# Attention's key sets joined pair by pair of heads, bias tables written from all partitions, last pair last in the branch product

## The chip, the cores and the metric

The kernel runs on one core of a Trainium2 chip. The metric is the device time of one execution in microseconds (us). Three executions were timed, and their median counts; one further execution was profiled.

## The reference, cut to what matters

The kernel computes two transformer blocks over 512 tokens of width 1024. The change lies in the attention branch of the first block. It has 24 heads: three groups of 8, whose keys lie 1, 4 and 16 tokens apart. The outputs of the three groups are joined by a softmax over their log denominators, head by head and token by token; a branch product and a gate follow.

```python
logits = einsum('znqhd,znkhd->znhqk', qb, kw) * HEAD_DIM ** -0.5 + bias   # bias by bucketed distance
m = max(logits); p = exp(logits - m); den = sum(p)
o = einsum('znhqk,znkhd->znqhd', p, vw) / den;  lse = m + log(den)
...
alpha = softmax(stack(lses, axis=2), axis=2)
attn = sum(alpha[..., None] * o, axis=2)                                  # 512 x 512
...
merged = gates[:, :, 0] * (attn @ w_attn_branch) + gates[:, :, 1] * (ssm @ w_ssm_branch)
```

## The kernel before

Products run in three passes (`mm3`, L301 to L303, and `tok`, L384 to L386), because each operand is split into a high and a low part. A weight block of 512 KB is loaded by SP's queue into `wraw` (3 buffers), ScalarE (ACT) makes the high part `whi` (L292) and VectorE (DVE) the low part `wlo` (L293); a block feeds 24 matmuls of 512 columns.

`attention` does this in order:

- `rel_bias` (L428) makes the bias tables. One small product gives a row of 384, 256 or 256 numbers for each of 8 heads, on 8 partitions. A transfer on GpSimd's (POOL's) queue writes each row 128 times to DRAM (`scr<-p`: 1536, 1024 and 1024 KB); another reads it back with a pitch one element shorter, which skews it into the table by query and key (`B<-scr`, into B0 and B12).
- The V projection takes 12 weight blocks `w_v` and 288 matmuls.
- `qk` projects queries and keys of one pair of heads: 6 blocks.
- `units` does the attention of one pair of heads: two key sets (`sid` 0 is the group of step 1; `sid` 1 holds the groups of steps 4 and 16 together, its queries in the order quarter by quarter, that is tokens 0, 4, 8, ..., then 1, 5, 9, ...), each in two halves. Scores and bias are added and their maximum taken (L483, DVE), exponents and sums made (L492, ACT), the weights transposed (L499, PE) and multiplied with V (L514). Maxima and sums go into `st`, outputs into `Os`. The units of pair hp are interleaved with `qk` of pair hp + 1; those of the last pair with 5 of the 8 gate blocks (`gates`, L828), which need nothing from attention.
- `attn_join` (L581) comes once, after all four pairs, interleaved with the remaining 3 gates. It transposes `st`, sends it to DRAM (`dstat`), reads it back with heads on 8 partitions (`R`), works out the weights `W` of the two sets on [8, 512] rows, sends them to DRAM (`dw`), reads them back copied over 64 partitions a head (`Wb<-dw`, 8 transfers of 256 KB), and forms y = Os0 * W0 + Os1 * W1 for each pair. L317 and L318 split y into `ah` and `al`. All its transfers are on SP's queue.

The branch product in `block1_` then takes four blocks `w_ab` of 24 matmuls, two output tiles each; every output tile needs `ah` and `al` of all four pairs. The order of instructions on each engine is made at build time by a list scheduler with a cost model of its own; each engine then runs its list strictly in order.

Of the kernel before, what the change touches and what calls it, by code (L numbers as in the profile page):

```python
# [10 lines left out]
F32 = mybir.dt.float32  # L11
# [7 lines left out]
P = 128  # L19
# [230 lines left out]
class Kern:  # L250
# [177 lines left out]
    def rel_bias(self, pool):  # L428

        nc, D = self.nc, self.D  # L430
        B0 = pool.tile([P, 8, 256], F32, name="B0", bufs=1)
        B12 = pool.tile([P, 8, 256], F32, name="B12", bufs=1)

        flat = lambda: pool.tile([P, 2, 2, 256], F32, name="p").rearrange("p a b c -> p (a b c)")
        tab, es = flat()[:NBUCKET + 1, :896], flat()[:8]
        nc.gpsimd.dma_start(tab, D["btab"])
        lhs = self.small.tile([NBUCKET + 1, 24], F32, name="lhs", bufs=1)
        nc.vector.memset(lhs[NBUCKET:NBUCKET + 1], 1.0)
        nc.gpsimd.dma_start(lhs[0:NBUCKET], D["relb"])
        off = 0  # L440
        for g, L in enumerate((384, 256, 256)):
            ps = self.btile()[:8, :L]
            nc.tensor.matmul(ps, lhs[:, g * 8:(g + 1) * 8], tab[:, off:off + L], start=True, stop=True)
            e = es[:, off:off + L]
            off += L
            nc.vector.tensor_copy(e, ps)
            scr = self.dram.tile([8, P * L + 512], F32, name="scr%d" % g)
            dst = scr[:, :P * L].rearrange("h (p l) -> h p l", l=L)
            nc.gpsimd.dma_start(dst, e.unsqueeze(1).to_broadcast([8, P, L]))
            src = scr[:, :P * (L - 1)].rearrange("h (p l) -> p h l", l=L - 1)  # L450
            if g == 0:
                nc.gpsimd.dma_start(B0, src[:, :, 0:256])
            else:
                nc.gpsimd.dma_start(B12[:, :, (g - 1) * P:g * P], src[:, :, 0:P])
        return B0, B12

    def attn_unit(self, pool, hp, sid, half, qT, kT, V, bias, st, O):
# [9 lines left out]
        for u in range(2):  # L467
# [13 lines left out]
            for e in range(2):  # L481
                h = 2 * hp + e
                nc.vector.tensor_tensor_reduce(p[:, e, u, lo:], S[e][:, u, lo:], bias[:, h, lo:], 1.0, -3e38,  # L483
                                               op0=ALU.add, op1=ALU.max, accum_out=st[:, 2 * sid, h, i:i + 1])
        mx = st[:, 2 * sid, 2 * hp:2 * hp + 2, 2 * half:2 * half + 2]
        nc.vector.tensor_scalar(ng.rearrange("p (e u) -> p e u", e=2), mx, -1.0, None, op0=ALU.mult)
        for u in range(2):
            i = 2 * half + u
            lo = P if sid == 0 and i == 0 else 0
            for e in range(2):  # L490
                h = 2 * hp + e
                nc.scalar.activation(p[:, e, u, lo:], p[:, e, u, lo:], AF.Exp, bias=ng[:, 2 * e + u:2 * e + u + 1],  # L492
                                     accum_out=st[:, 2 * sid + 1, h, i:i + 1])
        yield
# [23 lines left out]
    def attention(self, xT, ah, al, other):  # L518
# [3 lines left out]
        with self.tc.tile_pool(name="ao", bufs=1) as op:  # L522
          st = op.tile([P, 4, 8, 4], F32, name="st")
          Os = op.tile([P, 4, 2, SEQ], F32, name="Os")
          with self.tc.tile_pool(name="at", bufs=2) as pool:
# [25 lines left out]

            def units(hp, qT, kT):

                last = None
                for sid in range(2):
                    O = self.psO.tile([P, SEQ], F32, name="pso")
                    for half in range(2):
                        u = self.attn_unit(pool, hp, sid, half, qT, kT, V, (B0, B12)[sid], st, O)
                        next(u)
# [11 lines left out]
            for hp in range(4):  # L571
                merge(units(hp, *qk_[hp]), qk(hp + 1, *qk_[hp + 1]) if hp < 3 else islice(other, 5))
          with self.tc.tile_pool(name="ac", bufs=2) as pool:
              merge(self.attn_join(pool, st, Os, ah, al), other)

    def attn_end(self, last, Os):
        _, hp, sid, half, O = last
        if half:
            self.nc.scalar.copy(Os[:, hp, sid], O)

    def attn_join(self, pool, st, Os, ah, al):  # L581

        nc = self.nc
        ps = self.btile()[:, :P]
        nc.tensor.transpose(ps, st.rearrange("p a b c -> p (a b c)"), self.ident)
        sT = pool.tile([P, P], F32, name="sT", bufs=1)
        nc.vector.tensor_copy(sT, ps)
        dst = self.dram.tile([4, 8, 4, P], F32, name="dstat")
        nc.sync.dma_start(dst.rearrange("a b c p -> (a b c) p"), sT)
        R = pool.tile([8, 4, SEQ], F32, name="R", bufs=1)  # L590
        nc.sync.dma_start(R, dst.rearrange("a b c p -> b a (c p)"))
        v = lambda i: R[:, i].rearrange("h (r i) -> h i r", r=4)
        n = lambda t: t.rearrange("h (i r) -> h i r", r=4)
        W = pool.tile([8, 2, SEQ], F32, name="W", bufs=1)
        tm = pool.tile([8, 2, SEQ], F32, name="tm", bufs=1)
        M, L = tm[:, 0], tm[:, 1]
        V_, S_ = nc.vector, nc.scalar
        yield
        V_.tensor_tensor(n(M), n(R[:, 0]), v(2), op=ALU.max)
        V_.tensor_tensor(W[:, 0], R[:, 0], M, op=ALU.subtract)  # L600
        V_.tensor_tensor(n(W[:, 1]), v(2), n(M), op=ALU.subtract)
        S_.activation(W, W, AF.Exp)
        V_.tensor_tensor(L, W[:, 0], R[:, 1], op=ALU.mult)
        V_.tensor_tensor(n(M), n(W[:, 1]), v(3), op=ALU.mult)
        V_.tensor_tensor(L, L, M, op=ALU.add)
        V_.reciprocal(L, L)
        V_.tensor_tensor(W, W, L.unsqueeze(1).to_broadcast([8, 2, SEQ]), op=ALU.mult)
        dw = self.dram.tile([8, 2, SEQ], F32, name="dw")
        nc.sync.dma_start(dw, W)
        yield  # L610
        for hp in range(4):
            Wb = pool.tile([P, 2, SEQ], F32, name="Wb")
            for e in range(2):
                nc.sync.dma_start(Wb[64 * e:64 * e + 64], dw[2 * hp + e].unsqueeze(0).to_broadcast([64, 2, SEQ]))
            y = pool.tile([P, SEQ], F32, name="ay")
            z = pool.tile([P, SEQ], F32, name="az")
            V_.tensor_tensor(y, Os[:, hp, 0], Wb[:, 0], op=ALU.mult)
            V_.tensor_tensor(n(z), Os[:, hp, 1].rearrange("d (r i) -> d i r", r=4), n(Wb[:, 1]), op=ALU.mult)
            V_.tensor_tensor(y, y, z, op=ALU.add)
            self.dump("attnT%d" % hp, y)  # L620
            self.split(ah[:, hp], al[:, hp], y)
            yield

# [228 lines left out]
    def block1_(self, keep, c1):  # L852
# [5 lines left out]
        with tc.tile_pool(name="b1", bufs=1) as pl:  # L858
# [13 lines left out]
            with tc.tile_pool(name="ahl", bufs=1) as ap_:  # L872
# [3 lines left out]
                with tc.tile_pool(name="gp", bufs=1) as gp:  # L876
                    gts = [gp.tile([P, SEQ], F32, name="g%d" % i) for i in range(8)]
                    self.attention(xT, ah, al, self.gates(xT, 0, gts))
                    for s in range(4):
                        w = self.wload(D["w_ab"], s, 1)  # L880
                        for j in range(2):
                            fb = 2 * s + j
                            ps = self.ptile()
                            self.feat(ps, w, 0, (ah, al), kbn=4, off=j * 512)
                            V_.tensor_tensor(gts[fb], ps, gts[fb], op=ALU.mult)
# [1363 lines left out]
```

## Time and profile before

| | us |
|---|---|
| three runs | 3434.73, 3446.86, 3446.99 |
| median | 3446.86 |
| profiled execution | 3435.72 |
| its span | 3433.8 |

The span is the time from the first to the last instruction in the trace; 1.9 us of the profiled execution lie outside it. PE is TensorE's matmuls and PEld its weight loads. [...] The bracket behind a row names the idle time before it and what ended that.

### The profile page before, as it was taken

What the parts mean: (1) busy time and instruction counts of PE and PEld (TensorE: products, weight loads), DVE (VectorE), ACT (ScalarE), POOL (GpSimd) and SP (SyncE); (2) the same over time, 40 slices, a digit from 0 to 9 for tenths busy, and PEclk for the clock granted to TensorE, in tenths of its full rate; (3) what the DMA queues carried; (4) which work ended last, traced back from release to release, by engine and by line L of the source; (5) the groups of instructions that cost most, each with busy time, mean ns of one, the idle gap of its engine ahead of it and who ended that gap; (6) DMA issues with size and microseconds to landing.
All of it is one profiled execution on the core that took longest, in us unless ns stands there. A gap on an engine that the chain in (4) does not pass through costs nothing.

```text
span 3433.8 us, 53206 instructions
## 1 busy us (share of the span) xinstructions
PE 3209.5 (93%) x21803; PEld 2567.3 (75%) x21803; DVE 2010.4 (59%) x3226; ACT 1383.1 (40%) x2294; POOL 226.9 (7%) x260
## 2 busy tenths in 40 slices
PE   6999799999889999889899999989999989899998
PEld 5877577777677788766577888767788767778887
DVE  2333567775645543556655656667565754766656
ACT  2233244342344442443344444446532444543323
POOL 0000000000100000022121121000000200000001
PEclk9999999999999999999899999999999989999999
DMA  7411343445444432434555544542322325232323
GB/s 135 128 62 62 109 140 128 135 148 177 148 138 136 128 111 98 139 119 119 151 164 164 169 160 137 177 168 89 108 95 92 133 95 172 89 105 92 98 92 111
DMA packets 216843, 430.96 MB, mean 126 GB/s; under 512 B 75426, under 2 KB 114546, under 8 KB 216344
## 3 DMA queue, kind: packets, MB, share of 16 engines
q1 hardware_dynamic: 193736, 370.09, 34.1%
q10 hardware_dynamic: 20464, 51.58, 4.0%
q0 software_dynamic: 2400, 5.90, 1.7%
q8 instruction: 171, 2.80, 0.3%
q14 instruction: 72, 0.59, 0.1%
HBM read 380.70 MB, written 46.79 MB: 124 GB/s over the span
## 4 chain that ended last, share of the span: by engine, by line
PE 77%; DVE 9%; DMA 7%; ACT 4%; issue 2%; POOL 0%; SPq 0%; ACTq 0%; POOLq 0%; DVEq 0%
PE psa L301 11%; PE psa L303 11%; PE psa L302 11%; PE psa L385 5%; PE psa L384 5%; PE psa L386 5%; PE pso L301 3%; PE pso L303 3%; PE pso L302 3%; DVE wlo L293 2%; DMA wraw<-in_w_v_dram 1%; PE psa L1552 1%; ACT whi L292 1%; PE psa L1562 1%; PE pso L1017 1%
## 5 line engine op out<-in xcount | busy, mean ns | idle before, releaser
L293 DVE TENSOR_TENSOR wlo<-wraw,whi 128x1024 fp32r<-128x1024 f32 x480 | 597.5, 1246 | 524.2 <-ACT whi L292 518.7
L292 ACT CAST whi<-wraw 128x1024 fp32r<-128x1024 f32 x482 | 503.7, 1046 | 773.0 <-PE psa L386 224.6
L301 PE MATMUL psa<-xh,wlo 128*128 128x512 f32 (+1 forms) x1760 | 693.3, 396 | 18.0 <-DVE wlo L293 10.7
L303 PE MATMUL psa<-xh,whi 128*128 128x512 f32 (+1 forms) x1760 | 684.7, 390 | 0.0
L302 PE MATMUL psa<-xl,whi 128*128 128x512 f32 (+1 forms) x1760 | 683.7, 389 | 0.0
L301 PEld LDWEIGHTS psa<-xh,wlo 128*128 128x128 f32 x1760 | 335.6, 192 | 97.6 <-DVE wlo L293 14.9
L303 PEld LDWEIGHTS psa<-xh,whi 128*128 128x128 f32 x1760 | 336.0, 191 | 72.7 <-issue 4.2
L302 PEld LDWEIGHTS psa<-xl,whi 128*128 128x128 f32 x1760 | 336.3, 191 | 71.6 <-issue 3.8
L1138 DVE SCALAR_TENSOR_TENSOR fc<-psa,f_cv,fc 128x441 f32<-128x441 f32 (+2 forms) x352 | 243.4, 692 | 41.4 <-ACT fc L1127 34.5
L301 PE MATMUL pso<-xh,wlo 128*128 128x256 f32 (+1 forms) x720 | 232.0, 322 | 0.6 <-ACT u L1445 0.5
L302 PE MATMUL pso<-xl,whi 128*128 128x256 f32 (+1 forms) x720 | 222.0, 308 | 1.0 <-DVE xl L347 1.0
L303 PE MATMUL pso<-xh,whi 128*128 128x256 f32 (+1 forms) x720 | 221.8, 308 | 0.0
L385 PE MATMUL psa<-wlo,ah 128*128 128x512 f32 x528 | 210.9, 399 | 2.8 <-DVE wlo L293 2.5
L384 PE MATMUL psa<-whi,al 128*128 128x512 f32 x528 | 209.0, 399 | 3.4 <-ACT whi L292 3.4
L386 PE MATMUL psa<-whi,ah 128*128 128x512 f32 x528 | 209.7, 398 | 0.0
L301 PEld LDWEIGHTS pso<-xh,wlo 128*128 128x128 f32 x720 | 137.0, 190 | 12.9 <-issue 1.7
L302 PEld LDWEIGHTS pso<-xl,whi 128*128 128x128 f32 x720 | 136.9, 190 | 9.6 <-DVE xl L347 1.6
L303 PEld LDWEIGHTS pso<-xh,whi 128*128 128x128 f32 x720 | 136.5, 190 | 8.2 <-issue 0.8
L384 PE MATMUL psa<-whi,xl 128*128 128x512 f32 x288 | 117.6, 410 | 19.3 <-ACT whi L292 16.0
L385 PEld LDWEIGHTS psa<-wlo,ah 128*128 128x128 f32 x528 | 99.0, 188 | 30.1 <-DVE wlo L293 6.3
L384 PEld LDWEIGHTS psa<-whi,al 128*128 128x128 f32 x528 | 98.8, 187 | 29.6 <-ACT whi L292 4.7
L385 PE MATMUL psa<-wlo,xh 128*128 128x512 f32 x288 | 117.2, 407 | 1.1 <-DVE wlo L293 1.1
(554 smaller groups left out, 5168.5 us busy)
## 6 DMA issues: line engine op xcount, KB each, us to landing
wraw<-in_f_up_dram SPq DMA_DIRECT2D x132, 512.0 KB, 3.8
wraw<-in_ada_w_dram SPq DMA_DIRECT2D x96, 512.0 KB, 3.6
wraw<-in_f_dn_dram SPq DMA_DIRECT2D x66, 512.0 KB, 3.5
wraw<-in_w_fi_dram SPq DMA_DIRECT2D x44, 512.0 KB, 3.5
wraw<-in_ab_f_dram SPq DMA_DIRECT2D x38, 512.0 KB, 3.8
wraw<-in_w_qk_dram SPq DMA_DIRECT2D x24, 512.0 KB, 3.7
wraw<-in_w_xbc_dram SPq DMA_DIRECT2D x24, 512.0 KB, 4.7
wraw<-in_c_f_dram SPq DMA_DIRECT2D x24, 512.0 KB, 4.3
```

Of the source, the lines that this page charges most:

```text
L292: nc.scalar.copy(hi, raw)
L293: (eng or nc.vector).tensor_tensor(lo, raw, hi.bitcast(F32), op=ALU.subtract)
L301: mm(ps, wl, xh, start=start, stop=False)
L302: mm(ps, wh, xl, start=False, stop=False)
L303: mm(ps, wh, xh, start=False, stop=stop)
L384: mm(ps, sl, wh[:, c], start=first and k == 0, stop=False)
L385: mm(ps, sh, wl[:, c], start=False, stop=False)
L386: mm(ps, sh, wh[:, c], start=False, stop=last and k == kbn - 1)
L1017: nc.tensor.matmul(ps[o:o + 32], self.cs[:, 4 * h + j, 22 - 2 * i:54 - 2 * i], raw[:, j * 256:(j + 1) * 256], start=h == 0, stop=h == 1, t ...
L1138: V_.scalar_tensor_tensor(o, pv[:, r0 + dr:r1 + dr, c0 + dc:c1 + dc], cw(i), o, op0=ALU.mult, op1=ALU.add)
L1552: mm(ps[h, d, b], Al[h, d, b], Tm[h, d, b], start=True, stop=True, tile_position=(64 * e, 64 * e))
L1562: mm(ps[h, d, b], lt[h, d, b], rt[h, d, b], start=True, stop=True, tile_position=(64 * e, 64 * e))
```

## The change

- Bias tables: the columns of the small product's stationary operand are repeated 16 times (`rep`), so the product gives every row on 16 partitions, 128 in all. Each partition then writes its row 8 times to DRAM. The bytes written and the reads behind them stay as they are.
- Join: `attn_join` is called once for each pair, with that pair's `st` and `Os` (two buffers), and runs interleaved with the next pair's units; the last one runs with the remaining gates. Four gates instead of five stand beside the last pair's units. The statistics of a pair lie on 8 partitions as (head, block of 128 tokens), so each DVE instruction has 128 columns rather than 512. Those of set 1 are reordered by quarters within each block while they are written to DRAM, in four transfers. The transfers to `dstat` go out from ACT's queue (five for each pair), the others (`R`, `dw`, two of `Wb`) from POOL's.
- Branch product: two steps of four output tiles. All four first take their products of pairs 0 to 2, then those of pair 3; the evacuation stays as it was.

```diff
...
-        tab, es = flat()[:NBUCKET + 1, :896], flat()[:8]
+        tab, es = flat()[:NBUCKET + 1, :896], flat()
...
+        rep = pool.tile([NBUCKET + 1, 24, 16], F32, name="pT", bufs=3)
+        nc.vector.tensor_copy(rep, lhs.unsqueeze(2).to_broadcast([NBUCKET + 1, 24, 16]))
...
-            ps = self.btile()[:8, :L]
-            nc.tensor.matmul(ps, lhs[:, g * 8:(g + 1) * 8], tab[:, off:off + L], start=True, stop=True)
+            ps = self.btile()[:, :L]
+            nc.tensor.matmul(ps, rep[:, g * 8:(g + 1) * 8].rearrange("k h r -> k (h r)"), tab[:, off:off + L], start=True, stop=True)
...
-            scr = self.dram.tile([8, P * L + 512], F32, name="scr%d" % g)
-            dst = scr[:, :P * L].rearrange("h (p l) -> h p l", l=L)
-            nc.gpsimd.dma_start(dst, e.unsqueeze(1).to_broadcast([8, P, L]))
+            scr = self.dram.tile([8, P * L], F32, name="scr%d" % g)
+            dst = scr.rearrange("h (r q l) -> (h r) q l", q=8, l=L)
+            nc.gpsimd.dma_start(dst, e.unsqueeze(1).to_broadcast([P, 8, L]))
...
-                                               op0=ALU.add, op1=ALU.max, accum_out=st[:, 2 * sid, h, i:i + 1])
-        mx = st[:, 2 * sid, 2 * hp:2 * hp + 2, 2 * half:2 * half + 2]
+                                               op0=ALU.add, op1=ALU.max, accum_out=st[:, 2 * sid, e, i:i + 1])
+        mx = st[:, 2 * sid, :, 2 * half:2 * half + 2]
...
-                                     accum_out=st[:, 2 * sid + 1, h, i:i + 1])
+                                     accum_out=st[:, 2 * sid + 1, e, i:i + 1])
...
-          st = op.tile([P, 4, 8, 4], F32, name="st")
-          Os = op.tile([P, 4, 2, SEQ], F32, name="Os")
+          st = op.tile([P, 4, 4, 2, 4], F32, name="st")
+          join = iter(())
...
-            def units(hp, qT, kT):
+            def units(hp, qT, kT, Os):
...
-                        u = self.attn_unit(pool, hp, sid, half, qT, kT, V, (B0, B12)[sid], st, O)
+                        u = self.attn_unit(pool, hp, sid, half, qT, kT, V, (B0, B12)[sid], st[:, hp], O)
...
-                merge(units(hp, *qk_[hp]), qk(hp + 1, *qk_[hp + 1]) if hp < 3 else islice(other, 5))
-          with self.tc.tile_pool(name="ac", bufs=2) as pool:
-              merge(self.attn_join(pool, st, Os, ah, al), other)
+                Os = op.tile([P, 2, SEQ], F32, name="Os", bufs=2)
+                merge(units(hp, *qk_[hp], Os), qk(hp + 1, *qk_[hp + 1]) if hp < 3 else islice(other, 4), join)
+                join = self.attn_join(op, hp, st[:, hp], Os, ah, al)
+          merge(join, other)
...
-            self.nc.scalar.copy(Os[:, hp, sid], O)
-    def attn_join(self, pool, st, Os, ah, al):
+            self.nc.scalar.copy(Os[:, sid], O)
+    def attn_join(self, pool, hp, st, Os, ah, al):
...
+        V_, S_, G_ = nc.vector, nc.scalar, nc.gpsimd
+        ps = self.btile()[:32, :P]
+        nc.tensor.transpose(ps, st.rearrange("p a e c -> p (a e c)"), self.ident)
+        sT = pool.tile([32, P], F32, name="sT")
+        S_.copy(sT, ps)
+        dst = self.dram.tile([4, 2, 4, P], F32, name="dstat%d" % hp)
+        S_.dma_start(dst[0:2].rearrange("a e c p -> (a e c) p"), sT[0:16])
+        for x in range(4):
+            S_.dma_start(dst[2 + x // 2, x % 2].rearrange("c (r i) -> r c i", r=4),
+                         sT[16 + 4 * x:20 + 4 * x].rearrange("r (c i) -> r c i", c=4))
+        yield
+        R = pool.tile([8, 4, P], F32, name="R")
+        G_.dma_start(R, dst.rearrange("a e c p -> (e c) a p"))
...
+        M = pool.tile([8, P], F32, name="M")
+        V_.tensor_tensor(n(M), n(R[:, 0]), v(2), op=ALU.max)
+        V_.tensor_tensor(R[:, 0], R[:, 0], M, op=ALU.subtract)
+        V_.tensor_tensor(v(2), v(2), n(M), op=ALU.subtract)
+        W = R.rearrange("h (s k) p -> h s k p", k=2)
+        S_.activation(W[:, :, 0], W[:, :, 0], AF.Exp)
...
+        V_.tensor_tensor(W[:, :, 1], W[:, :, 0], W[:, :, 1], op=ALU.mult)
+        V_.tensor_tensor(n(M), n(R[:, 1]), v(3), op=ALU.add)
+        V_.reciprocal(M, M)
+        V_.tensor_tensor(R[:, 0], R[:, 0], M, op=ALU.mult)
+        V_.tensor_tensor(v(2), v(2), n(M), op=ALU.mult)
+        dw = self.dram.tile([2, 2, 4, P], F32, name="dw%d" % hp)
+        G_.dma_start(dw.rearrange("s e c p -> (e c) s p"), W[:, :, 0])
...
+        Wb = pool.tile([P, 2, SEQ], F32, name="Wb")
+        for e in range(2):
+            G_.dma_start(Wb[64 * e:64 * e + 64], dw[:, e].rearrange("s c p -> s (c p)").unsqueeze(0).to_broadcast([64, 2, SEQ]))
+        yield
+        y, z = Os[:, 0], Os[:, 1]
+        V_.tensor_tensor(y, y, Wb[:, 0], op=ALU.mult)
+        zv = z.rearrange("d (r c i) -> d r c i", r=4, c=4)
+        V_.tensor_tensor(zv, zv, Wb[:, 1].rearrange("d (c r i) -> d r c i", r=4, c=4), op=ALU.mult)
+        yv = y.rearrange("d (i r) -> d i r", r=4)
+        V_.tensor_tensor(yv, yv, z.rearrange("d (r i) -> d i r", r=4), op=ALU.add)
+        self.dump("attnT%d" % hp, y)
+        self.split(ah[:, hp], al[:, hp], y)
+        yield
...
-                    for s in range(4):
-                        w = self.wload(D["w_ab"], s, 1)
-                        for j in range(2):
-                            fb = 2 * s + j
-                            ps = self.ptile()
-                            self.feat(ps, w, 0, (ah, al), kbn=4, off=j * 512)
+                    for s in range(2):
+                        w = self.wload(D["w_ab"], 2 * s)
+                        pss = [self.ptile() for _ in range(4)]
+                        for j, ps in enumerate(pss):
+                            self.feat(ps, w, j // 2, (ah, al), kbn=3, off=j % 2 * 512, last=False)
+                        for j, ps in enumerate(pss):
+                            fb = 4 * s + j
+                            self.feat(ps, w, j // 2, (ah, al), kbn=1, kbx=3, off=j % 2 * 512 + 384, first=False)
...
```

## Rows read from the trace of the kernel before

**Rows 1.** The page: busy time of the span, and the chain that ended last.

```profile
PE 3209.5 (93%) x21803; PEld 2567.3 (75%) x21803; DVE 2010.4 (59%) x3226; ACT 1383.1 (40%) x2294; POOL 226.9 (7%) x260
...
PE 77%; DVE 9%; DMA 7%; ACT 4%; issue 2%; POOL 0%; SPq 0%; ACTq 0%; POOLq 0%; DVEq 0%
```

**Rows 2.** PE's waits, 18 to 420 us: total, times, longest, in us.

```profile
PE psa L384 <- ACT whi L292: 16.0, 1, 16.0
...
PE psa L301 <- ACT ah L317: 15.2, 2, 15.0
```

**Rows 3.** Waits of all engines, 0 to 160 us.

```profile
ACT whi L292 <- DMA wraw<-in_w_v_dram: 46.0, 5, 30.5
...
POOL B L452 <- DMA scr<-p: 53.1, 1, 53.1
```

**Rows 4.** Stretches: engine busy us (x instructions), PEclk, DMA share, GB/s.

```profile
30.00:40.00 10.00, 10.00 (x46) 8.26 (x44) 2.45 (x2) 1.40 (x2) 0.00 (x0) 1.00 0.95 55
...
116.00:160.00 44.00, 44.00 (x193) 35.81 (x191) 12.41 (x11) 10.15 (x11) 0.00 (x0) 0.98 0.32 108
...
43.20:56.90 13.70, 13.69 (x59) 13.01 (x57) 1.93 (x3) 0.00 (x0) 0.00 (x0) 1.00 0.97 56
...
55.31:114.10 58.79, 38.54 (x152) 36.05 (x151) 12.76 (x14) 8.62 (x9) 3.71 (x5) 0.85 0.79 155
...
114.10:117.85 3.75, 3.75 (x9) 2.93 (x10) 2.87 (x4) 0.82 (x1) 0.44 (x1) 0.54 0.89 283
...
368.68:383.62 14.94, 0.00 (x0) 0.00 (x0) 7.77 (x8) 2.12 (x3) 0.00 (x0) 0.67 0.50 141
...
383.62:408.71 25.09, 24.73 (x97) 18.54 (x97) 17.59 (x23) 5.01 (x6) 0.00 (x0) 0.93 0.51 161
```

**Rows 5.** DMA issues: form, queue, count, KB each, median us to landing.

```profile
scr<-p POOLq DMA_DIRECT2D x1, 1536.0 KB, 55.0
...
B<-scr POOLq DMA_DIRECT2D x1, 1024.0 KB, 8.0
...
lhs<-in_relb_dram POOLq DMA_DIRECT2D x1, 3.0 KB, 6.3
...
Wb<-dw SPq DMA_DIRECT2D x8, 256.0 KB, 4.6
...
lad<-tmp ACTq DMA_DIRECT2D x1, 64.0 KB, 1.6
...
Cd<-C ACTq DMA_DIRECT2D x1, 2056.0 KB, 7.5
```

**Rows 6.** ACT's timeline, 344 to 436 us: start, us, what.

```profile
424.43 0.33 ACTq L650 DMA_DIRECT2D tmp<-in_resets_dram  x1
```

**Rows 7.** DVE's timeline, 344 to 436 us.

```profile
353.75 0.29 DVE L587 COPY sT<-psb 128x128 f32<-128x128 f32 x1 [1.86 <-PE pso L514]
...
360.48 1.07 DVE L599 TENSOR_TENSOR tm<-R 8x512 f32<-8x512 f32 x1
...
368.23 3.34 DVE L606 RECIPROCAL tm<-tm 8x512 f32<-8x512 f32 x1
...
380.56 0.69 DVE L617 TENSOR_TENSOR ay<-Os,Wb 128x512 f32<-128x512 f32 x1 [6.45 <-DMA Wb<-dw]
```

**Rows 8.** The chain that ended last, 340 to 440 us: start, us, what.

```profile
373.00 1.79 DMA dw<-W
...
382.95 0.63 ACT ah L317
```

**Rows 9.** PE's timeline at the end of the last unit.

```profile
348.07 0.50 PE L301 MATMUL psa<-xh,wlo 128*128 128x512 f32 x1
...
352.31 0.33 PE L585 MATMUL psb<-masks,st 128*128 128x128 f32 x1
```

**Rows 10.** A stretch of 52 us with the units of one pair.

```profile
215.00:267.00 52.00, 51.67 (x287) 38.26 (x286) 18.37 (x49) 19.86 (x47) 0.31 (x1) 1.00 0.19 62
```

More of the change, by code (lines that the diff above doesn't have):

```diff
@@ L578, in attn_end @@
         if half:
-            self.nc.scalar.copy(Os[:, hp, sid], O)
-    def attn_join(self, pool, st, Os, ah, al):
+            self.nc.scalar.copy(Os[:, sid], O)
+    def attn_join(self, pool, hp, st, Os, ah, al):
         nc = self.nc
[L584 to L591, printed above, removed]
+        V_, S_, G_ = nc.vector, nc.scalar, nc.gpsimd
[11 more added lines that the diff above has]
+        G_.dma_start(R, dst.rearrange("a e c p -> (e c) a p"))
@@ L592, in attn_join @@
         v = lambda i: R[:, i].rearrange("h (r i) -> h i r", r=4)
         n = lambda t: t.rearrange("h (i r) -> h i r", r=4)
[L594 to L597, printed above, removed]
-        yield
-        V_.tensor_tensor(n(M), n(R[:, 0]), v(2), op=ALU.max)
-        V_.tensor_tensor(W[:, 0], R[:, 0], M, op=ALU.subtract)
-        V_.tensor_tensor(n(W[:, 1]), v(2), n(M), op=ALU.subtract)
@@ L602, in attn_join @@
[L602 to L609, printed above, removed]
-        yield
[L611 to L622, printed above, removed]
+        M = pool.tile([8, P], F32, name="M")
```

## Prediction

> **What bounds the kernel now.** I read the page first. PE is busy 93% of the span, and the chain that ended last runs through PE for 77% [rows 1]. So a change of order pays only where PE stands still. PE's waits over the stretch that the change touches come second: two of them stand out, 16.0 us for a `whi` in the V projection and 15.0 us for `ah` ahead of the branch product [rows 2]. The change meets both places, so each is traced to its cause.
>
> The first wait. The `whi` casts had waited 46.0 us in all for V's weight blocks, 30.5 us of it once, while POOL waited 53.1 us for `scr<-p` [rows 3]. In the stretches, the DMA engines are 95% to 97% busy and move only 55 and 56 GB/s [rows 4]: the tables' 1536 KB needed 55.0 us [rows 5] beside the 1024 KB behind it. Those transfers read 8 partitions. For comparison, `Cd<-C` writes 2056 KB to DRAM from 128 partitions in 7.5 us [rows 5]. The weight blocks share the engines with these slow transfers and starve.
>
> The second wait. Gates cover the join until 368.68, then PE stands for 14.94 us [rows 4]. The join's steps can be read off: statistics in SBUF at 353.75 + 0.29, first DVE instruction on `R` at 360.48, first product with `Wb` at 380.56 [rows 7], `ah` from 382.95 for 0.63 [rows 8].
>
> **The change part by part.**
>
> *Bias tables, gain.* From 55.31 to 114.10 PE did 152 matmuls; at the rate just before (13.69 us for 59, 0.232 each) they take 35.3 us of 58.79 [rows 4]: 23.5 lost. The restart after it ran 9 matmuls in 3.75 us with PEclk 0.54; at 0.228 (44.00 for 193) they take 2.1 [rows 4]: 1.7 more. Together 25.2. How much comes back depends on the price of the new write. Nearest row for its 128 partitions to DRAM: 7.5 us for 2056 KB, so 5.6 for 1536 KB; nearest for POOL's queue with 1-KB pieces: `B<-scr`, 1024 KB in 8.0 [rows 5], so 12.0. The first two tables, 2560 KB, then need 9 to 20 us instead of 55. A weight block must land within what three `wraw` buffers cover, 3 x 24 x 0.232 = 16.7 us, and it gets a share of the engines meanwhile; I take all 25.2 as returned. Lower end: transfers only twice as fast, about half, 12.
>
> The added `rep` copy, 128 instead of 8 columns in three small stationary loads, and three evacuations of more partitions but equal columns are tenths of a us in a stretch where DVE is busy 2.45 of 10 us [rows 4]; without that cover they cost under 1 us.
>
> *Last join, gain.* The old exposure is 14.94 of standing and, in the 25.09 us of the branch product, what exceeds 96 x 0.228 = 21.9 (late `ah` of one pair after another, half clock): 3.2. Together 18.1 [rows 4].
> The number of gates is the same, so they end at 368.68 on the old clock; the sixth gate's matmuls stand among the last unit's even now (348.07) [rows 9], so that four instead of five gates beside the units leave no hole. Then 36 matmuls of pairs 0 to 2 take 8.2 us. Pair 3's `ah` is wanted at 376.9, that is 22.9 us after the statistics (354.04).
> Its chain: five issues on ACT at 0.33 [rows 6] are 1.7, landing 1.6 as `lad<-tmp` from ACT [rows 5]: 3.3. `R` on POOL's queue: no small POOL transfer under quiet conditions is shown; between 1.6 (`lad`) and 6.3 (`lhs`, 3 KB, issued amid the first loads) [rows 5]. I take 3.0, nearer the first since the DMA engines are mostly free there. Arithmetic: four columns of the old ones are one now; 1.07 becomes 0.27 to 0.4, the reciprocal 3.34 [rows 7] becomes 0.84; eight DVE steps and an exponent come to about 3.9, with one `wlo` between them 5.1. `dw`: 1.79 on SP [rows 8] to 6.3; 3.0. `Wb`: two transfers of 256 KB, 4.6 on SP [rows 5] to 8.0 + 0.9 on POOL; 5.3. Products, sum and `ah`: 380.56 to 383.58 before [rows 7, 8], 3.0, plus 0.4 as the sum is now strided: 3.4. Sum 3.3 + 3.0 + 5.1 + 3.0 + 5.3 + 3.4 = 23.1, so PE waits 0.2 us; I put 1.0 for the semaphores between. Both ends: low 3.3 + 1.6 + 3.9 + 1.8 + 4.6 + 3.4 = 18.6, hidden; high 3.3 + 6.3 + 5.1 + 6.3 + 8.9 + 3.4 = 33.3, late by 10.4 plus 1.7 for a slow restart, 12.1. Gain 17.1, between 6.0 and 18.1.
>
> [...]
>
> *Joins beside the units, cost.* Three more transposes, 0.33 each [rows 9]: 1.0. In a pair's 52 us DVE is busy 18.37 and ACT 19.86, PE 51.67 [rows 10]. A join adds about 4 + 4 us to DVE and 2.5 to ACT, which fits. But DVE waits in order for `R` and `Wb`, with scores (L483), `pT` copies and `wlo` queued behind it, and PE behind those; ACT's five issues stand ahead of exponents. Each step comes a round of the interleaving later, some 6 us, so I take 1 us a pair, 3.0; nothing at best (0), 6.3 + 6.3 + 8.9 = 21.5 a pair if DVE stands through the whole of `R`, `dw` and `Wb`: 64.5.
>
> *Branch product, regrouped.* 96 matmuls and 8 evacuations as before. The second step needs the first's tiles evacuated, each free while PE finishes the next ones (3 x 0.228 each against 0.69 for an evacuation): nothing, at most 1 us.
>
> **Sum.** -25.2 - 17.1 + 1.0 + 3.0 = -38.3. Against the profiled execution's own 3435.7 that gives 3397. Of the three runs one lies at that level (3434.7) and two, with the median, 12 us above (3446.9); from the median the sum gives 3409. I say 3403.
>
> **Rivals.** *Tables stay slow*: the rate belongs to the queue or the pieces, not to 8 partitions. Against it, `B<-scr` runs on the same queue at 131 GB/s. For it, source rows are still read repeatedly. Without the first gain: 3436 to 3447 - 13, 3423 to 3434; about 3428.
> *The last join comes late*: POOL's hops at the high end. For it, only `lhs` is a small POOL transfer and it took 6.3. 11 us dearer: 3414.
> *Slower*: POOL's hops at the high end, and DVE, in order, stands at `R` and `Wb` through them in every pair, 64.5 us. -25.2 - 6.0 + 1.0 + 64.5 = +34.3, 3470 to 3481. It outweighs the gains once a pair stalls over (25.2 + 6.0 - 1.0) / 3 = 10.1 us. Against it: DVE idles 33 of 52 us, and a join's steps lie a round apart, so that other work of DVE stands between a transfer and its use.
> [...]
>
> **How the numbers follow.** Forecast 0.75 (3388 to 3418 by itself), late join 0.11, slow tables 0.09, slower 0.05. A measurement of this kernel tells about 0.5%, 17 us, from no change: faster is below 3429.6. The forecast and the late join fall there, and half of the slow tables: 0.90; the other half and a little of the slower case, where stalls just eat the gains, make no difference: 0.06; slower 0.04. The range goes from 3388 (all 43 us from the low level, and a little) to 3428 (slow tables, or half of both gains from the upper level).
>
> **What would show it.** After: `scr<-p` landing in 6 to 15 us; DMA below 90% busy from 30 to 60 us; no PE wait over 3 us and full clock up to the first unit, which comes some 25 us earlier. A gap ahead of pair 3's part of the branch product under 3 us. PE as busy beside the units as now; `R` and `Wb` absent from DVE's long waits. The prediction is wrong if `whi` still waits for `w_v`, if DVE's waits for `R` or `Wb` reach several us a pair, or if POOL's transfers land in 6 us or more.

## The result, and the profile after

| | before | after |
|---|---|---|
| runs | 3434.73 to 3446.99 | 3394.08 to 3406.89 |
| median | 3445.33 (4 runs) | 3401.34 (4 runs) |
| profiled execution | 3435.72 | 3406.89 |

The ratio is 0.9877, with a 95% interval from 0.985 to 0.9905. The kernel became 1.2% faster; 3403 was predicted, with a range from 3388 to 3428. The profiled execution of after is the slowest of its four, that of before lies near the fast end of its runs; so the two traces differ by 28.8 us and the medians by 44.0.

The page of after answers to [rows 1]:

```profile
PE 3215.0 (94%) x21806; PEld 2578.7 (76%) x21806; DVE 2013.4 (59%) x3250; ACT 1383.3 (41%) x2301; POOL 236.0 (7%) x276
...
PE 78%; DVE 9%; DMA 6%; ACT 4%; issue 2%; POOL 0%; SPq 0%; ACTq 0%; POOLq 0%; DVEq 0%
```

As much work as before stands in a shorter span. PE's waits from 18 to 390 us (total, times, longest) answer to [rows 2]:

```profile
PE psa L301 <- DVE MT L318: 5.9, 1, 5.9
PE psa L482 <- DVE st L486: 3.1, 5, 1.7
PE psa L301 <- ACT ah L317: 0.5, 1, 0.5
```

Both large waits of before are gone, 16.0 us for `whi` and 15.2 for `ah`. At the top stands a wait that the prediction does not name: 5.9 us for `MT`, the split weights of the time-step projection, which comes right behind the branch product. The kernel before has that wait too, 2.3 us long, under the name "issue": it ends at the first matmul with `MT`, just after VectorE has made the low part of `MT` (PE's and DVE's timelines of before: start, us, what):

```profile
416.57 0.39 PE L301 MATMUL psa<-xh,MT 128*32 128x512 f32 x1 [2.26 <-issue]
```

```profile
416.04 0.43 DVE L318 TENSOR_TENSOR MT<-MT 128x256 fp32r<-128x256 f32 x1
```

**The tables.** DMA issues from 0 to 160 us (count, KB, median us to landing) and two stretches (busy us and count of PE, PEld, DVE, ACT, POOL; PEclk, the share of full speed granted to TensorE's clock; DMA share, GB/s) answer to [rows 4, 5]:

```profile
scr<-p POOLq DMA_DIRECT2D x2, 1024.0 KB, 10.7
scr<-p POOLq DMA_DIRECT2D x1, 1536.0 KB, 7.3
B<-scr POOLq DMA_DIRECT2D x1, 1024.0 KB, 10.0
```

```profile
30.00:40.00 10.00, 10.00 (x46) 8.27 (x45) 2.45 (x2) 1.70 (x2) 0.92 (x1) 1.00 1.02 339
40.00:50.00 10.00, 10.00 (x46) 9.03 (x45) 5.04 (x6) 2.10 (x2) 2.09 (x3) 1.00 0.96 340
```

The 1536 KB land in 7.3 us instead of 55.0. The DMA engines are as busy as before (a share of 1.02 from 30 to 40 us, where it was 0.95), but they move 339 GB/s where they moved 55. So the share alone did not tell the two kernels apart here, and the bytes did. One sign that the prediction gave did not come for that reason: the DMA engines were to be below 90% busy from 30 to 60 us, and the shares are 1.02, 0.96 and, only in the last 10 us, 0.48.

**The last join.** DVE's timeline (start, us, what, [idle before <- what ended it]) and the chain that ended last (start, us, what):

```profile
329.99 0.38 DVE L606 TENSOR_TENSOR M<-R 8x128 f32<-8x128 f32 x1
...
336.70 0.37 DVE L616 TENSOR_TENSOR R<-R,M 8x128 f32<-8x128 f32 x1
...
348.11 0.69 DVE L625 TENSOR_TENSOR Os<-Os,Wb 128x512 f32<-128x512 f32 x1 [3.45 <-DMA Wb<-dw]
...
350.45 1.10 DVE L629 TENSOR_TENSOR Os<-Os 128x512 f32<-128x512 f32 x1
```

```profile
337.66 2.64 DMA dw<-R
...
341.48 6.54 DMA Wb<-dw
...
351.58 0.63 ACT ah L317
...
368.46 4.17 DMA accd<-g
372.76 0.37 ACTq L639
```

The statistics leave PSUM (the memory that PE writes its results to) at 323.78 + 0.25 = 324.03, and `ah` is ready at 352.20: the chain takes 28.2 us.

**The new wait.** ACT's timeline at the end of the branch product, and SP's:

```profile
372.76 0.37 ACTq L639 DMA_DIRECT2D hc<-in_hcol_dram  x1
373.39 0.78 ACT L698 ACTIVATE cacc<-psa,convb,conv 128x512 f32<-128x512 f32 x1 [5.66 <-DMA accd<-g]
373.42 0.37 ACTq L641 DMA_DIRECT2D MT<-in_w_dt_dram  x1
```

```profile
365.36 1.68 SPq L899 DMA_DIRECT2D accd<-g  x3
...
368.46 0.32 SPq L899 DMA_DIRECT2D accd<-g  x1
```

An evacuation takes a finished tile out of PSUM, here with the multiplication by the gate (L898); a store `accd` (L899) then sends it to DRAM. The second step of the branch product ends with four of each in a row. The last store lands some 4.2 us after its issue; ACT's queue, which is to load `hc` and the time-step weights next, stands until then; from those weights' load to PE's first matmul with them (377.96) another 4.5 us pass. After this stand PE restarts with PEclk at 0.50. By the starts on PE's timeline a matmul of 512 columns then takes 0.43 us (four from 378.36 to 380.07), and 0.23 us once PEclk is back at 1.00 (ten from 381.79 to 384.12):

```profile
375.00:380.00 5.00, 2.04 (x5) 0.86 (x6) 3.55 (x5) 1.24 (x4) 0.00 (x0) 0.50 0.30 108
380.00:385.00 5.00, 5.00 (x20) 2.33 (x19) 0.00 (x0) 0.00 (x0) 0.00 (x0) 0.87 0.00 0
```

**Where the time came from, by stage.** Where each stage ends in every profile of this study, in us, told by the start of one instruction: the first evacuation of `qk` (all tables and V done), the last gate on ACT, the last evacuation of the branch product, the time-step addition behind it, the span, and what lies between the last two. That rest has the same instructions in the same order in all of them, but for a few at its start in the two with the ring.

| profile | qk | gates | branch | time step | span | rest |
|---|---|---|---|---|---|---|
| before | 121.5 | 368.6 | 408.9 | 422.3 | 3433.8 | 3011.5 |
| before, again | 123.7 | 372.1 | 412.7 | 427.4 | 3438.3 | 3010.9 |
| after | 96.5 | 343.6 | 367.7 | 385.2 | 3405.1 | 3019.9 |
| tables alone | 95.8 | 340.1 | 380.9 | 395.9 | 3410.6 | 3014.7 |
| all but tables | 123.9 | 370.1 | 394.2 | 412.9 | 3423.2 | 3010.3 |
| old branch product | 95.4 | 339.6 | 366.9 | 380.0 | 3402.2 | 3022.2 |
| second step by tiles | 94.5 | 338.7 | 361.5 | 374.9 | 3387.9 | 3013.0 |
| time-step weights in ring | 94.1 | 338.1 | 360.9 | 372.4 | 3383.0 | 3010.6 |
| joins on SP | 93.8 | 336.5 | 359.3 | 377.3 | 3390.7 | 3013.4 |
| ring and SP | 96.2 | 338.9 | 360.9 | 372.7 | 3388.0 | 3015.3 |
| five gates | 96.0 | 342.3 | 365.1 | 383.5 | 3394.4 | 3010.9 |
| 16 partitions | 93.4 | 341.2 | 365.8 | 383.7 | 3397.6 | 3013.9 |
| 32 partitions | 93.8 | 340.5 | 364.3 | 381.6 | 3404.8 | 3023.2 |

After leads by 25.0 us at the first projection, 25.0 at the gates' end, 41.2 at the branch product's end, 37.1 at the time step, and 28.7 at the end. The last 8.4 us are not traced to the change: the rest takes 3010.3 to 3023.2 us from one profile to another, and both 3010.9 (five gates) and 3023.2 (32 partitions) come from the kernel after with small edits far ahead of the rest. What the trace shows for them is PE's busy time over the same matmuls, in before and in after (the rest as one stretch, columns as above):

```profile
422.30:3433.80 3011.50, 2841.72 (x20004) 2280.94 (x20003) 1849.71 (x2921) 1250.18 (x2036) 217.66 (x243) 0.97 0.40 129
```

```profile
385.20:3405.10 3019.90, 2852.82 (x20004) 2293.51 (x20003) 1850.83 (x2921) 1249.76 (x2036) 217.88 (x243) 0.97 0.40 129
```

PE is busy 11.1 us longer with the same work, while DVE and ACT differ by about 1 us or less. Reckoned as time at PEclk 0.50 (twice what PEclk lacks to 1.00, added up over the rest), the clock was at half for 159 us in before and for 191 in after; in the profile with 32 partitions, the longest rest, for 201. It is not the whole of it (176 us with the old branch product, whose rest is 3022.2), and why one execution is granted less than another no run here shows. So stages are compared below within the traces, and whole times by the timed runs.

### The profile page after: what moved, and what is told of

Same layout as the page of the kernel before. It is cut to its first block, busy times and chain, and to the rows that moved or that the text cites. A ratio compares the mean times of both kernels' runs of the same rounds, so it can differ in the third digit from the quotient of the medians.

```text
span 3405.1 us, 53304 instructions
## 1 busy us (share of the span) xinstructions
PE 3215.0 (94%) x21806; PEld 2578.7 (76%) x21806; DVE 2013.4 (59%) x3250; ACT 1383.3 (41%) x2301; POOL 236.0 (7%) x276
## 4 chain that ended last, share of the span: by engine, by line
PE 78%; DVE 9%; DMA 6%; ACT 4%; issue 2%; POOL 0%; SPq 0%; ACTq 0%; POOLq 0%; DVEq 0%
PE psa L301 11%; PE psa L303 11%; PE psa L302 11%; PE psa L385 6%; PE psa L386 6%; PE psa L384 6%; PE pso L301 3%; PE pso L302 3%; PE pso L303 3%; DVE wlo L293 2%; PE psa L1565 1%; PE psa L1575 1%; PE pso L1030 1%; ACT whi L292 1%; DMA wraw<-in_f_up_dram 1%
## 5 line engine op out<-in xcount | busy, mean ns | idle before, releaser
L301 PE MATMUL psa<-xh,wlo 128*128 128x512 f32 (+1 forms) x1760 | 696.7, 398 | 15.2 <-DVE wlo L293 11.9
L301 PEld LDWEIGHTS psa<-xh,wlo 128*128 128x128 f32 x1760 | 337.9, 193 | 95.5 <-DVE wlo L293 15.3
L386 PEld LDWEIGHTS psa<-whi,ah 128*128 128x128 f32 x528 | 99.2, 188 | 23.3
```

The source lines that it names most:

```text
L301: mm(ps, wl, xh, start=start, stop=False)
L386: mm(ps, sh, wh[:, c], start=False, stop=last and k == kbn - 1)
```

## Experiments

**1. Tables alone, and all but the tables.** The first is the kernel before with the new `rel_bias`; the second is the kernel after with the old one.

```diff
-        tab, es = flat()[:NBUCKET + 1, :896], flat()[:8]
+        tab, es = flat()[:NBUCKET + 1, :896], flat()
...
+        rep = pool.tile([NBUCKET + 1, 24, 16], F32, name="pT", bufs=3)
...
-            dst = scr[:, :P * L].rearrange("h (p l) -> h p l", l=L)
+            dst = scr.rearrange("h (r q l) -> (h r) q l", q=8, l=L)
```

> The kernel before with the new bias tables alone; join and branch product as before. Theory, two separate gaps of PE: scr<-p of 1536 KB lands in about 7 us, PE's 16.0-us wait for whi in the V projection is gone and the first query-key block comes 25 us earlier, while PE still stands some 15 us ahead of the branch product; the time is 25 us below the kernel before. Rival, the two gains are one (the earlier start only moves waiting to the join): the stand ahead of the branch product grows by 10 us or more and under 12 us are gained.

> The changed kernel with the old bias tables (8 source partitions); join by pairs and regrouped branch product stay. Theory: the 16-us wait in the V projection is back, the join's gain of 17 us at the end of the branch product stays, and the later wait of 6 us for the step-size weights (tile MT) stays too, so the time is 12 us below the kernel before (17 less some 5) and 25 us above the changed kernel. Rival, the changed kernel's gain is mostly the join's: within 15 us of the changed kernel.

Tables alone: median 3408.61, ratio 0.9905 [0.988, 0.9929], 32.7 us of before's 3444, where 25 were expected; the interval goes from 24 to 41. All but the tables: 3433.67, ratio 0.997 [0.9953, 0.9986], 10.3 us, where 12 were expected; the interval goes from 5 to 16. Together 43.0, and the whole change gave 0.0123 x 3444 = 42.4: within these intervals the parts add, and both theories held against their rivals. PE's waits from 18 to 430 us, first with the tables alone, then without them:

```profile
PE psa L301 <- ACT ah L317: 16.0, 3, 15.6
```

```profile
PE psa L384 <- ACT whi L292: 16.6, 1, 16.6
PE psa L301 <- DVE MT L318: 5.8, 1, 5.8
```

Each wait goes with its own part. In the stages, the tables alone bring the first projection 25.7 us forward; the rest of the change brings gates' end to time step from 53.7 us to 42.8. The new `MT` wait belongs to the second part.

**2. The branch product of before in the kernel after.**

```diff
-                    for s in range(2):
-                        w = self.wload(D["w_ab"], 2 * s)
-                        pss = [self.ptile() for _ in range(4)]
...
+                    for s in range(4):
+                        w = self.wload(D["w_ab"], s, 1)
+                        for j in range(2):
...
+                            self.feat(ps, w, 0, (ah, al), kbn=4, off=j * 512)
```

> The changed kernel with the old branch product, two tiles a block, each with all four pairs in order. Theory: the first tile asks for pair 3 after 9 matmuls instead of 36, so PE stands about 6 to 7 us instead of 0.5 there, while evacuations and stores spread out again and the later wait for MT falls from 5.9 to about 2 us; about 2 us above the changed kernel. Rival, the regrouping has no part in the wait for MT: it stays at 5 to 6 us and the time is 7 us above.

3395.71, ratio 0.9863 [0.9831, 0.9895]: not to be told from the kernel after. PE's waits say why:

```profile
PE psa L301 <- ACT ah L317: 3.6, 1, 3.6
PE psa L301 <- issue: 2.0, 1, 2.0
```

Without the regrouping pair 3's `ah` is wanted earlier and PE waits 3.6 us for it. 6 to 7 were expected, as if 9 matmuls stood ahead of pair 3's first; in this kernel's list it is 21 (339.39 to 343.93 on PE), because the scheduler draws products of other tiles forward by itself, and with the regrouping 36. The branch product ends 27.3 us after the gates instead of 24.1. In return the wait for `MT` is back at the 2 us of the kernel before. It stands under "issue", but it is the same wait: it ends at the first matmul with `MT`, right after its low part is made (PE, DVE):

```profile
374.29 0.39 PE L301 MATMUL psa<-xh,MT 128*32 128x512 f32 x1 [2.04 <-issue]
```

```profile
373.77 0.42 DVE L318 TENSOR_TENSOR MT<-MT 128x256 fp32r<-128x256 f32 x1
```

From the branch product's end to the time step pass 13.1 us instead of 17.5. So the regrouping wins 3.2 us at its front and loses 4.4 at its end; by the time step it has cost about 1 us, which is within what a single trace can tell.

**3. Two cures of the new wait.** The first regroups only the first step and does the second tile by tile, so that its evacuations and stores spread. The second leaves the products alone and puts the time-step weights into the ring of weight blocks, loaded by SP.

```diff
+                            if s == 0:
+                                self.feat(ps, w, j // 2, (ah, al), kbn=1, kbx=3, off=j % 2 * 512 + 384, first=False)
+                            else:
+                                self.feat(ps, w, j // 2, (ah, al), kbn=4, off=j % 2 * 512)
```

> The kernel after with the second step of the branch product tile by tile (all four pairs of one output tile, then the next); the first step stays regrouped. Theory, that PE's wait of 5.9 us for the split time-step weights comes from the four evacuations and stores of the second step falling in the last 4 us of the branch product: the last store goes out as soon as before, but the three ahead of it are done by then, so the wait is 2 to 3 us as in the kernel before, and the time-step addition comes 3 to 4 us after the place it has relative to the gates' end now (41.6 us after the gates becomes 38). Rival, that the wait belongs to the load of those weights on ACT's queue whatever the evacuations do: 5 to 6 us again.

```diff
-        raw = tmp.tile([P, 256], F32, name="MT", bufs=3)
-        nc.scalar.dma_start(raw, D["w_dt"])
-        hi = tmp.tile([P, 8, 32], F32R, name="MT", bufs=3)
+        raw = self.wp.tile([P, 1024], F32, name="wraw")[:, :256]
+        nc.sync.dma_start(raw, D["w_dt"])
+        hi = self.wp.tile([P, 1024], F32R, name="whi")[:, :256].rearrange("p (a b) -> p a b", a=8)
...
```

> The changed kernel with the step-size weights loaded by SP into the ring of weight blocks (wraw, whi, wlo), so that their place does not depend on the gates' stores. PE's order is the same. Theory, the wait for MT is the wait of its load for the last stores accd<-g: PE's wait of 5.9 us there falls below 1 us, the clock stays full, and the next stage comes about 5 us earlier. Rival, PE would wait there anyway (for a free tile in PSUM or a block of w_xbc): a wait of 3 us or more stays under another name.

Second step by tiles: one execution, 3389.65. The wait for `MT` is down to 2.3 us, as the theory had it; it stands under "issue" again and ends at the first matmul with `MT` (369.14). The time step comes 36.2 us after the gates instead of 41.6; 38 was expected. Behind the shorter wait PEclk stays at 1.00 in each 5 us from 365 to 375, where the wait of 5.9 us brought it to 0.50. PE's waits in this run:

```profile
PE psa L301 <- issue: 2.3, 1, 2.3
PE psa L482 <- DVE st L486: 1.9, 4, 1.3
```

In the ring PE has no wait at that place: 3387.95 (3384.83 to 3391.68), ratio 0.9847 [0.9818, 0.9875]; all its runs lie below all those of the kernel after, and the time step comes 34.3 us after the gates. PEclk is 1.00 in each 5 us from 355 to 380. Both cures work, each by another end of the same chain. Spreading the stores brings the wait back to what it was before the change; taking the load out from behind them removes it. That ACT's queue waits because the loads' buffers lie where the stored tiles were is what the code suggests; it was not tried by itself.

**4. One gate block less of cover.**

```diff
-                merge(units(hp, *qk_[hp], Os), qk(hp + 1, *qk_[hp + 1]) if hp < 3 else islice(other, 4), join)
+                merge(units(hp, *qk_[hp], Os), qk(hp + 1, *qk_[hp + 1]) if hp < 3 else islice(other, 5), join)
```

> The kernel after with five instead of four gate blocks beside the last pair's units, so that three instead of four stand between the last statistics and the branch product. Theory, that the last join is hidden only because its cover (27.6 us from the statistics to the place where ah is wanted) happens to equal its length (28.2): one gate block less is 24 matmuls, 5.5 us less of cover, so PE waits some 5 us for ah (3 to 6, as a shorter queue of casts and tanh may shorten the chain by 1 to 2), and the half-clock restart adds 1 to 2. Rival, that the length follows the cover, because the steps of the chain stand behind the gates' casts and tanh on ACT and DVE: a wait under 2 us.

The theory fell: PE doesn't wait for `ah` at all, and the one execution took 3396.18. The statistics are out at 326.33 + 0.25, 2.6 us later than in the kernel after, yet `ah` is ready at 349.63, 2.6 us earlier. DVE's timeline and ACT's:

```profile
334.16 0.38 DVE L606 TENSOR_TENSOR M<-R 8x128 f32<-8x128 f32 x1
...
338.02 0.38 DVE L616 TENSOR_TENSOR R<-R,M 8x128 f32<-8x128 f32 x1
...
346.56 0.69 DVE L625 TENSOR_TENSOR Os<-Os,Wb 128x512 f32<-128x512 f32 x1 [1.44 <-DMA Wb<-dw]
```

```profile
326.33 0.25 ACT L593 COPY sT<-psb 32x128 f32<-32x128 f32 x1 [0.41 <-PE psb L591]
...
349.01 0.62 ACT L317 CAST ah<-Os 128x512 fp32r<-128x512 f32 x1 [5.14 <-DVE Os L629]
```

The chain takes 23.1 us here and 28.2 in the kernel after: the arithmetic 4.2 instead of 7.1, `dw` and `Wb` 8.2 instead of 11.0, the products and the cast 3.1 instead of 4.1; only the way to `R` is longer, 7.6 instead of 6.0. The arithmetic and the products are a matter of order. In the kernel after the exponent (L610) stands behind a gate's tanh (L838) in ACT's list, and ACT waits 3.9 us for that gate's matmuls; two `wlo` stand between the steps on DVE:

```profile
332.71 0.60 ACT L838 ACTIVATE g<-psa 128x512 f32<-128x512 f32 x1 [3.90 <-PE psa L303]
333.21 0.40 ACT L610 ACTIVATE R<-R 8x256 f32<-8x256 f32 x1
```

The 2.8 us of `dw` and `Wb` are something else: the transfers themselves land sooner (`dw` 1.7 instead of 2.6 us, `Wb` 4.1 to 4.6 instead of 6.2 to 6.5), and why is not shown. The rival held in its number, a wait under 2 us. Its reason, that the steps stand behind other work on ACT and DVE, covers 3.9 us; 2.8 come from the transfers, and the longer way to `R` takes 1.6 back. So the chain's length is no constant against which to hold the cover.

**5. The joins' transfers on SP's queue.** All `dma_start` of `attn_join` by SP:

```diff
-        S_.dma_start(dst[0:2].rearrange("a e c p -> (a e c) p"), sT[0:16])
+        nc.sync.dma_start(dst[0:2].rearrange("a e c p -> (a e c) p"), sT[0:16])
...
-        G_.dma_start(R, dst.rearrange("a e c p -> (e c) a p"))
+        nc.sync.dma_start(R, dst.rearrange("a e c p -> (e c) a p"))
```

> The kernel after, with all transfers of the joins on SP's queue (dstat, R, dw, Wb), where SP also issues the weight blocks in order. Theory, that the queue matters: each hop lands about as soon as from POOL (R 2.4, dw 1.7, Wb 5.1 us there; 1.8 to 4.6 from SP in the kernel before), but SP stands at each of them until the join's DVE steps are done, the weight blocks behind it go out late, and PE waits for whi several us in every pair: 5 to 20 us slower than the kernel after. Rival, that the three buffers of weight blocks cover those stands: within 5 us of the kernel after, and the hop for Wb is not shorter than 4 us either way, since its 256 KB set it.

3395.45, ratio 0.9859 [0.9827, 0.989]: not slower, and not to be told from the kernel after. The theory fell. DVE's wait for `Wb` from 140 to 345 us, first in the kernel after, then here:

```profile
DVE Os L625 <- DMA Wb<-dw: 16.0, 3, 6.2
```

```profile
DVE Os L625 <- DMA Wb<-dw: 9.2, 4, 3.2
```

SP does stand at the joins' steps (39.0 us in four waits for `sT`, 14.2 in four for the arithmetic on `R`), but the three weight buffers cover it: PE waits for no `whi`. DVE's stands become shorter, and PE's waits for `st` are 0.6 us, where the traces with the four joins on POOL's queue and the new tables have 1.8 to 3.3 us.

> The kernel after with both edits that were seen to help: the time-step weights in the weight ring, loaded by SP, and the joins' transfers on SP's queue. Theory, that they act at different places (PE's 5.9 us wait with its half-clock restart behind the branch product; DVE's stands at the joins' weights beside the units) and add: to the kernel after -13.5 and -6, so about 3382, span 3376 to 3388, ratio to before 0.982 to 0.984. Rival, that both only bring forward the same later work and that time is set behind them: no better than the better one alone, 3388.

This edit and the ring together: 3391.35, ratio 0.9847 [0.9826, 0.9868], the ratio of the ring alone. The rival held; what the shorter stands give is below what can be measured.

**6. Fewer source partitions.** The kernel after with 2 and with 4 copies of the columns instead of 16:

```diff
-        rep = pool.tile([NBUCKET + 1, 24, 16], F32, name="pT", bufs=3)
+        rep = pool.tile([NBUCKET + 1, 24, 2], F32, name="pT", bufs=3)
...
-            dst = scr.rearrange("h (r q l) -> (h r) q l", q=8, l=L)
+            dst = scr.rearrange("h (r q l) -> (h r) q l", q=64, l=L)
```

> The kernel after, with the stationary columns repeated 2 times instead of 16, so that the rows of the bias tables lie on 16 partitions and each is written 64 times to DRAM; queue, bytes and the reads behind stay. Theory, that the rate goes with the number of source partitions: the first two tables (2560 KB) ran at 47 GB/s from 8 partitions, so 94 GB/s from 16, and both have landed some 28 us after the first issue; the DMA engines stay over 90% busy meanwhile and a wait of PE for a weight block of V of several us remains. Rival, that the 8 partitions were slow only because one source row was read 128 times in a row, so that any spreading cures most of it: both land within 18 us, no such wait.

> As the run with 16 partitions, with the columns repeated 4 times: 32 partitions, each row written 32 times. Theory, rate by source partitions: 188 GB/s, both first tables landed some 14 us after the first issue, as fast as from 128 (13.5 us, where the bytes become the bound), and no wait of PE for V's blocks over 3 us. Rival, that the rate goes on rising up to 128 partitions: some 20 us or more.

DMA issues, with 16 partitions and with 32:

```profile
scr<-p POOLq DMA_DIRECT2D x2, 1024.0 KB, 22.9
scr<-p POOLq DMA_DIRECT2D x1, 1536.0 KB, 20.1
```

```profile
scr<-p POOLq DMA_DIRECT2D x2, 1024.0 KB, 13.3
scr<-p POOLq DMA_DIRECT2D x1, 1536.0 KB, 12.8
```

From the first issue until POOL goes on behind the landing of both first tables pass 58.0 us with 8 partitions (27.63 to 85.59), 31.6 with 16 (24.82 to 56.38), 18.1 with 32 (25.17 to 43.31) and 13.5 with 128 (27.75 to 41.28). For 2560 KB that is 45, 83, 145 and 194 GB/s: near doubling at first, less later. With 16 partitions that is near the theory (28 us) and far from the rival (under 18); with 32 it lies between theory (14) and rival (20 or more). One thing these runs cannot separate: with more partitions each row is read fewer times (128, 64, 32 and 8 times), so the rate may hang on the partitions or on the repeats. The queue and the bytes written are the same in all. Nor is it shown that the bytes become the bound at 128, as the expectation for 32 had it.

The rest of the expectation for 16 partitions came only in part: the DMA engines stay 96% to 99% busy from 30 to 60 us and ACT still waits up to 12.5 us for a block of V, but no wait of PE for one is left. And 3399.36 and 3406.54 (one execution each) lie among the times of the kernel after.

**7. The kernel before once more.**

> The kernel before, unchanged, for a second profile of it. It shows by how much the times of stages differ between two executions of one kernel. Expected: the wait of PE for a weight block of V again 15 to 17 us and the one for ah 14 to 16 us, the first unit's evacuation within 3 us of 121.5, and the stretch after the branch product, where all kernels have the same instructions, different by up to 12 us.

Its waits are the same, 16.0 for `whi` and 15.3 for `ah`; the stages come 2 to 5 us later, and the rest takes 3010.9, as expected. What a single trace tells of a stage is good to a few us.

## Why the prediction was right, step by step

**Tables, -25.2.** Right: -25.0 at the first projection, 25.7 with the tables alone. What it rests on held too: with the same queue and the same bytes, the rate went from 45 GB/s to 83, 145 and 194 as the rows were spread over 16, 32 and 128 source partitions instead of 8 (and each was read fewer times). The two first tables needed 13.5 us, within 9 to 20. The lower bound was wrongly reasoned: a rate only twice as high was to bring half (12 us), but 16 partitions, at 83 GB/s instead of 45, bring all; ACT still waits for weight blocks there, up to 12.5 us, and PE does not.

**Joins beside the units, +3.0, and transposes, +1.0.** The lead is 25.0 us on both sides of the units, so no net cost shows; it is within the few us by which that stretch scatters (242.7 to 248.4 us between the same two marks). The stands that the prediction feared exist: DVE waits 6.2 us for `Wb` at worst and 16.0 in three joins, over 5 us each. By the prediction's own sign ("several us a pair") this part was wrong: `Wb` was to be absent from DVE's long waits, and no transfer of POOL was to take 6 us, which `Wb` took in the last join (6.2 to 6.5). The cost did not follow, for PE loses little of it, 3.1 us in all for `st`; the longest is this wait of 1.7 us at 258.33 with the clock down behind it:

```profile
255.00:260.00 5.00, 3.28 (x21) 2.41 (x20) 3.28 (x10) 0.96 (x1) 0.00 (x0) 0.84 0.00 1
260.00:265.00 5.00, 5.00 (x19) 4.05 (x20) 3.15 (x6) 2.60 (x9) 0.00 (x0) 0.82 0.25 88
```

The slower rival needed 10.1 us of PE's time in every pair. DVE's stands reached half of that, PE's nothing near it.

**Last join, -17.1.** From the last gate to the last evacuation of the branch product the time fell from 40.3 to 24.1 us, 16.2; PE's wait for `ah` is 0.5. The sum was right, its two sides were not. The chain took 28.2 us instead of 23.1: the arithmetic 7.1 where 5.1 was taken, `dw` and `Wb` with POOL's issues 11.0 where 8.3 was, the products and the cast 4.1 where 3.4 was (the strided sum alone 1.10 us instead of 0.69, as the 0.4 for it had it), and the way to `R` 6.0 where 6.3 was. The 1.0 for the semaphores was the author's estimate, and no run shows it by itself. And pair 3's `ah` was wanted 27.6 us after the statistics instead of 22.9, because with four gates instead of five beside them the last units end earlier against the gates; the prediction held the statistics at their old place. The run with five gates has that place (15.8 us from the statistics to the last gate, 19.6 in the kernel after), and there the chain takes the 23.1 us forecast and is hidden too. So it is luck that the two errors cancel in the number; that the join is hidden is not, as the run with five gates has it too.

POOL's hops, in the kernel after from 140 to 345 us (count, KB, median us to landing):

```profile
Wb<-dw POOLq DMA_DIRECT2D x8, 256.0 KB, 5.1
...
R<-dstat POOLq DMA_DIRECT2D x4, 16.0 KB, 2.4
dw<-R POOLq DMA_DIRECT2D x4, 8.0 KB, 1.7
```

2.4 + 1.7 + 5.1 = 9.2 us for the three hops by their medians; the prediction took 11.3, its upper end 21.5. In the last join itself they took 2.2, 2.6 and up to 6.5, so 11.3.

**Branch product regrouped, "nothing, at most 1 us".** This is the step that failed. It counted matmuls and evacuations of the product, but not what is queued behind its last stores. The lead falls from 41.2 to 37.1 us there. Four evacuations and stores fall together at the end, ACT's queue waits for the last store to land, and PE then waits 5.9 us for the weights that ACT loads; with every tile of the last step evacuated by itself that wait is 2.0 to 2.3 us, before the change and after it, and with the weights in the ring it is gone. The front of the regrouping is worth about half of what the sum supposed: by the place where pair 3's `ah` is wanted it should save 27 matmuls, 6.2 us; the scheduler puts 21 ahead without it, so 15 are saved, and 3.2 us.

**The sum.** -38.3 was forecast and -37.1 stands at the time step. That they agree so well is luck in part: the regrouping took back 4.1 that the joins and transposes, at +4.0, did not cost. The timed runs give -42.4, with an interval from -33 to -52 that holds -37.1, and the two traces -28.7; the rest of the kernel scatters by more than these differences. That 3403 lies 2 us from the median 3401.34 says no more either: the four runs lie between 3394 and 3407.

## What to carry to other kernels

Where DMA engines are nearly all busy and move few bytes, as here with a share of 0.95 at 55 GB/s, look at how few partitions the transfer reads and how often it reads each row; doubling the first and halving the second was enough here (31.6 us for two tables instead of 58.0, and no wait of PE). Whoever moves evacuations to the end of a stage has to look at what the next stage loads into, and on which queue: here four stores in a row made PE's wait for the next loads 5.9 us instead of 2.3. And a chain's length measured under one cover does not tell the slack: here its steps took other places in the order of the engines when the cover changed, and it took 28.2 us under four gates and 23.1 under three. A wait that a view calls "issue" may still be a wait for data, as the 2.3 us for `MT` were here: look at what the first instruction behind it reads.

## What was not expected of the hardware

The rate of a transfer from SBUF (the on-chip memory) to DRAM went 45, 83, 145 and 194 GB/s with 8, 16, 32 and 128 source partitions, at a DMA share of 0.95 to 1.02 each time from 30 to 50 us. And the same instructions of the remaining 3010 us took up to 13 us more in some executions; in the two longest with the regrouped branch product PE was busy 11 to 13 us longer with the same matmuls, and the clock stood at half for 191 and 201 us instead of 159.
